# One weight unit converted earlier, two accumulating weight units fewer, and another schedule for the modulation weights, in a four-layer fp32 decoder trunk

## The chip, the cores and the metric

One core of a Trainium2 chip runs the whole program. The metric is device microseconds of one execution. The engines are named as in the profile: PE (TensorE), PEld (its weight loads), DVE (VectorE), ACT (ScalarE), POOL (GpSimd) and SP (SyncE, which here issues most of the DMAs).

## What is computed

`x` is (1, 256, 1024) in float32, `c` is (1, 1024). Four layers, each a token mixer followed by a causal convolution FFN; the mixers are gMLP, latent attention (MLA), HGRN2 (a gated recurrence) and gMLP again.

```
mod = silu(c) @ ada_w[l] + ada_b[l]           # 6 x 1024 per layer: shift, scale, gate, twice
h = rmsnorm(x, mix_norm_g[l]) * (1 + scale1) + shift1
x = x + gate1 * mixer(h)
h = rmsnorm(x, ffn_norm_g[l]) * (1 + scale2) + shift2
x = x + gate2 * ((silu(gate) * val) @ w_down)   # gate, val = split(conv3(h @ w_up))
# gMLP: z = gelu(h @ w_in); u, v = split(z); v = layernorm(v)
#       y = u * (tril(w_s) @ v + b_s); out = y @ w_out
# HGRN2: q, f, i, g = split(h @ w_in); chunked gated recurrence over q, 1-f, i; rmsnorm * silu(g); @ w_o
```

The result is rmsnorm of the last x.

## The kernel before, in words

**Products.** Every large product runs on PE as three fp32r matmuls: the weight is split into `wh` (the fp32r rounding) and `wl` (the rest), the activation into `hh` and `hlo`, and wh·hh, wl·hh and wh·hlo are summed (`mm3`, L252). Weights come in units of 128x2048 floats (1 MB). SP issues each unit's DMA (L190) into one of five `raw` buffers in the order of a list (`plan`), and `conv_half` (L194) splits it by halves: ACT casts a half to `wh` (L215), DVE subtracts to get `wl` (L223). The last arguments of `want` mark units as `again`: for the first half of those, no subtract runs on DVE; ACT multiplies by -1 (L220) and POOL issues a DMA that adds the weight again from memory into `wl` (L221, 512 KB). `unit(ahead, more)` (L227) hands the next unit to the product that asks, after issuing DMAs and conversions up to `ahead` (default 3) units on.

**Stages.** The gMLP of layer 0 begins with the first product: eight K chunks, each one `unit(1, 0)`, for three 512-column blocks of v (`proj_tok_first`, L731), whose results go through ACT's Gelu (`sink`, L792); the fourth block of v (units 8 and 9) follows, then squares (L807), a product of the gate weights (`rsum`, L830; `wsp`, L851), the eight u units with the gate products `sv` (L871), and the eight `go` units back to 1024 columns. Each FFN has 22 `up` units and 11 `dn` units. Where a norm follows, the last chunks of the product before it are held back (`tokens`, L632; `out_end`, L611): DVE applies gates and adds to x (`early`, `gated`, L547 and L548), ACT squares, and PE can begin the transposes `xt` (L495) of the next stage when the scaled row is there (`gx`, L483). On DVE's list `early` stands behind the subtracts of the units that were converted ahead. In HGRN2 a chain of eight levels runs on ACT and DVE (`qk`, `hp`, `hs`, L1208 to L1221), whose products `gram` (L1166, 64 short matmuls a level) run on PE between the products of the i and g units, and DVE copies them (L1168).

**Modulation.** `mod` of the later layers is computed in between. A piece (l, u) is 1024 of the 6144 columns and has four quarters of 1 MB. The pieces of the list `ADA_P` go to PE (quarter: DMA L323, 16 matmuls, L337), the others to DVE (DMA L353, two multiply-and-sum instructions, L362). `pace` (L239) sets for each stage two rates from the table `RATE`, (PE, DVE): how many quarters are loaded for each weight unit; `pacing` (L430) loads them, and runs a loaded quarter two units later. Near the end of a product it loads quarters for the norm instead, as many as `GAPS` says, and `modulated` (L524) runs some of them on PE behind the product. All quarters and units go through SP's one list, in the order in which the code was written out.

Of the kernel before, what the change touches and what calls it, by code (L numbers as in the profile page):

```python
# [22 lines left out]
KC = D // P  # L23
# [21 lines left out]
HGF = 1  # L45
HGO = "o0 o1 s0 a0 o2 s1 a1 n0 o3 s2 n1 w0 s3 n2 w1 n3 w2 w3"
HOLD = (3, 4)
ADA_P = [(1, 1), (1, 2), (1, 3), (1, 4), (2, 3), (2, 4), (3, 5)]
ADA_D = [(l, u) for l in range(L) for u in range(6) if (l, u) > (0, 1) and (l, u) not in ADA_P]
RATE = {("mix", 0): (0.05, 0.9), ("u", 0): (0.1, 1.0), ("go", 0): (0.35, 0.5), ("up", 0): (0.1, 0.2),  # L50
        ("dn", 0): (0.0, 0.4), ("mix", 1): (2.0, 0.0), ("up", 1): (0.0, 0.32), ("dn", 1): (0.0, 0.97),
        ("mix", 2): (0.0, 0.0), ("lev", 2): (0.5, 0.0), ("hout", 2): (0.25, 0.0), ("up", 2): (0.0, 0.2),
        ("dn", 2): (0.0, 0.87), ("mix", 3): (0.0, 0.5), ("u", 3): (0.0, 0.6), ("go", 3): (0.0, 0.55),
        ("up", 3): (0.0, 0.0), ("dn", 3): (0.0, 0.0)}
MAGIC = 12582912.0
TWO_PI = 2.0 * math.pi
# [35 lines left out]
def build(ctx, tc, A, out, stages=None):  # L92
# [62 lines left out]
    i = act.activation(cact[:], cin[:], AF.Silu)  # L155
# [15 lines left out]
    def want(aps, again=()):  # L171

        plan.extend((*a, i in again) for i, a in enumerate(aps))
# [53 lines left out]
    def unit(ahead=None, more=DMA_AHEAD):  # L227
        u = state["use"]
        ahead = state["ahead"] if ahead is None else ahead
        while state["dma"] < min(len(plan), u + ahead + (more if u else 0)):  # L230
            dma_next()
        while state["conv"] < min(len(plan), u + ahead) or halves:
            conv_half()
        state["use"] += 1
        r = ready.pop(0)
        pacing()
        return r

    def pace(kind, l, left=None, tag=None):  # L239
        state["rate"] = dict(zip("pd", RATE[kind, l]))  # L240
        state["gap"] = GAPS[2 * l + (kind in ("up", "dn"))]
        if left is not None:
            state["left"] = left
        if tag is not None:
            state["tag"] = tag
# [72 lines left out]
    def ada_tensor(l, u):  # L318


        def load(i):
            raw = ada_tile(f"adaw{l}_{u}_{i}", (P, 2, 4, 256))
            nc.sync.dma_start(raw[:].rearrange("p a b c -> p (a b c)"), A["adap"][ADA_P.index((l, u)), i])  # L323

            def run():
                h = ADA_P.index((l, u)) % 2
                ps = adaps[:, h, :]
# [44 lines left out]
    firsts = {}  # L372
# [358 lines left out]
    def proj_tok_first(name, sink, start=None):  # L731

        nb = 3 if start else 2
        ps = [(acc if i < 4 else misc)(f"{name}{i}") for i in range(2 * nb)]

        def part(w, b, e):
            return w[b // 2][e][:, b % 2 * 512 : b % 2 * 512 + 512]

        def chunk(kc):
            if start:  # L740
                firsts["w"] = unit(1, 0)
            elif kc % 2 == 0:
                firsts["w"] = unit(2)
            with contextlib.ExitStack() as es:
                if start and kc < KC - 1:
                    es.enter_context(tc.issue_after(firsts["pe"]))
                w = firsts["w"] if start else firsts["w"][kc % 2 :]
                if not start:
                    if kc:
                        low(kc - 1, firsts["wp"])  # L750
                    firsts["wp"] = w
                for b in range(nb):
                    for t in range(2):
                        for e in range(2):
                            i = pe.matmul(ps[2 * b + t][:], hh[:, kc, t * P : t * P + P], part(w, b, e), start=kc == 0 and e == 0, stop=False)  # L755
                if start or kc == KC - 1:
                    i = low(kc, w)
            firsts["pe"] = state["mm"] = getattr(i, "ins", i)

        def low(kc, w):  # L760
            for b in range(nb):
                for t in range(2):
                    i = pe.matmul(ps[2 * b + t][:], hlo[:, kc, t * P : t * P + P], part(w, b, 0), start=False, stop=kc == KC - 1)
            return i

        if start:
            start(chunk)
        else:
            for kc in range(KC):
                chunk(kc)  # L770
        for i in range(2 * nb):
            sink(i // 2, i % 2, ps[i])
# [324 lines left out]

    def hg_units():
        for n in ("hg_f", "hg_q", "hg_i", "hg_g", "hg_o"):
            want([(A[n][i], 2048) for i in range(4)], {"hg_f": (0, 1), "hg_i": range(4), "hg_g": range(4)}.get(n, ()))  # L1100

    def hg_bounds():
        lbp = prm[:, col("lb") : col("lb") + 32].rearrange("p (d h) -> p d h", d=4)
# [280 lines left out]
    for t in range(2):  # L1384
        act.activation(ss0[:, 6 + t : 7 + t], ss0[:, t : t + 1], AF.Sqrt, bias=epsc[:], scale=1.0 / D)
        scaled(t, root(t, ss0[:, 6:8]))
    for m, units in (("p", ADA_P), ("d", ADA_D)):
        for l, u in units:
# [61 lines left out]
def pack(i):  # L1450
# [36 lines left out]
    ap = aw.reshape(L, 4, 2, P, 6, 8, 4, 32)  # L1487
    r["adap"] = np.stack([ap[l, :, :, :, u].transpose(0, 2, 1, 4, 3, 5).reshape(4, P, 2048) for l, u in ADA_P])

# [52 lines left out]
```

## Time and profile before

| | |
|---|---|
| median of 3 runs | 1368.1 us (1364.61, 1368.1, 1368.23) |
| the profiled execution, and its span | 1369.07 us, 1367.3 us |
| PE busy | 1323.5 us (97%) |
| DVE, ACT, POOL busy | 1105.1, 799.6, 37.7 us |
| DMA | 340.16 MB, 249 GB/s on average |
| mean granted PE clock | 0.989 |

PE is busy nearly throughout, so what it waits for, and where its clock is at half, is read place by place. The stages begin at about (us from the span's start): first product 13, u 76, go 132, up of layer 0 185, dn 324, MLA 380, up of layer 1 472, dn 599, HGRN2 670, up of layer 2 829, dn 973, gMLP of layer 3 1022, up 1173, dn 1299.

### The profile page before, as it was taken

How to read it: one execution, taken by the hardware profiler on the slowest of the kernel's cores; microseconds unless marked ns; L12 is line 12 of the kernel's file. 1: busy time of each engine (PE TensorE's matmuls, PEld its weight loads, DVE VectorE, ACT ScalarE, POOL GpSimd, SP SyncE). 2: the span in 40 equal slices, each digit the busy share in tenths (PEclk: the TensorE clock that was granted, in tenths of full speed). 3: DMA queues.
4: the chain of work that ended last, by engine and by line, in shares of the span. 5: the costliest groups of instructions: out<-in, count | busy, mean ns of one | idle time of the engine just before them, and what ended most of it. 6: DMA issues, size and time to landing. Idle time of an engine off the chain costs nothing. (4 is left out here: it accounts for less than half of the span.)

```text
span 1367.3 us, 25166 instructions
## 1 busy us (share of the span) xinstructions
PE 1323.5 (97%) x10197; PEld 1202.2 (88%) x10197; DVE 1105.1 (81%) x1851; ACT 799.6 (58%) x1252; POOL 37.7 (3%) x47
## 2 busy tenths in 40 slices
PE   8999989999999999999898999999999999999997
PEld 7789889998878799988796879999778998999986
DVE  4499869899776689899866867899988896888874
ACT  4664456665376666653596556666455754666652
POOL 0000000000000000000011000000000000000000
PEclk9999999999999999999999999999999999999999
DMA  9868976666985466589769474657878589355550
GB/s 374 314 231 302 382 252 224 230 221 230 397 312 205 151 217 232 204 339 374 273 202 297 136 244 147 217 208 295 321 295 328 209 312 367 118 178 184 200 200 31
DMA packets 52188, 340.16 MB, mean 249 GB/s; under 512 B 6884, under 2 KB 8036, under 8 KB 13926
## 3 DMA queue, kind: packets, MB, share of 16 engines
q1 hardware_dynamic: 48320, 326.95, 63.8%
q0 software_dynamic: 2592, 9.44, 3.7%
q10 hardware_dynamic: 1160, 2.17, 0.5%
q8 instruction: 80, 1.31, 0.4%
q14 instruction: 36, 0.29, 0.1%
HBM read 337.45 MB, written 1.08 MB: 248 GB/s over the span
## 5 line engine op out<-in xcount | busy, mean ns | idle before, releaser
L215 ACT CAST wh<-raw 128x1024 fp32r<-128x1024 f32 (+1 forms) x422 | 429.4, 1041 | 323.7 <-PE up L706 89.3
L223 DVE TENSOR_TENSOR wl<-raw,wh 128x1024 fp32r<-128x1024 f32 (+1 forms) x404 | 483.5, 1213 | 105.8 <-ACT wh L215 105.3
L705 PE MATMUL up<-hh,wh 128*128 128x256 f32 x1280 | 314.2, 283 | 0.0
L706 PE MATMUL up<-hlo,wh 128*128 128x256 f32 x1280 | 314.1, 283 | 0.0
L705 PEld LDWEIGHTS up<-hh,wh 128*128 128x128 f32 x1280 | 245.7, 192 | 0.4 <-ACT y L1334 0.4
L706 PEld LDWEIGHTS up<-hlo,wh 128*128 128x128 f32 x1280 | 245.7, 192 | 0.0
L709 PE MATMUL up<-hh,wl 128*128 128x256 f32 x1280 | 179.8, 283 | 0.0
L709 PEld LDWEIGHTS up<-hh,wl 128*128 128x128 f32 x1280 | 165.1, 192 | 0.4 <-issue 0.4
L362 DVE CUSTOM_DVE_ANT_0 adaw<-adaw,cbc,prm 128x1024 f32<-128x1024 f32 x120 | 151.2, 1279 | 5.3 <-DMA adaw<-adad 5.3
L254 PE MATMUL dn<-wl,gh 128*128 128x512 f32 x339 | 133.3, 393 | 2.3 <-DVE wl L223 2.3
L1334 ACT ACTIVATE y<-up,cwb 128x256 f32<-128x256 f32 x176 | 98.8, 561 | 60.4 <-DVE y L1336 60.4
L253 PE MATMUL dn<-wh,gh 128*128 128x512 f32 x339 | 130.1, 390 | 1.4 <-DVE y L1336 1.3
L255 PE MATMUL dn<-wh,gl 128*128 128x512 f32 x339 | 131.0, 389 | 0.0
L1335 DVE SCALAR_TENSOR_TENSOR y<-up,cwb,y 128x255 f32<-128x255 f32 x176 | 84.4, 479 | 25.6 <-ACT y L1334 25.0
L1336 DVE SCALAR_TENSOR_TENSOR y<-up,cwb,y 128x254 f32<-128x254 f32 x176 | 84.0, 477 | 1.4
L254 PEld LDWEIGHTS dn<-wl,gh 128*128 128x128 f32 x339 | 63.6, 188 | 19.0 <-DVE wl L223 6.4
L253 PEld LDWEIGHTS dn<-wh,gh 128*128 128x128 f32 x339 | 63.7, 188 | 15.2 <-ACT warm L630 1.7
L255 PEld LDWEIGHTS dn<-wh,gl 128*128 128x128 f32 x339 | 63.7, 188 | 12.9
L705 PE MATMUL u<-hh,wh 128*128 128x256 f32 x256 | 64.5, 290 | 0.0
L706 PE MATMUL u<-hlo,wh 128*128 128x256 f32 x256 | 62.9, 283 | 0.0
L653 ACT CAST gh<-g 128x256 fp32r<-128x256 f32 x88 | 35.3, 401 | 37.2 <-DVE g L1341 36.6
L654 DVE TENSOR_TENSOR gl<-g,gh 128x256 fp32r<-128x256 f32 x88 | 37.1, 422 | 20.7 <-ACT gh L653 18.7
(388 smaller groups left out, 2258.2 us busy)
## 6 DMA issues: line engine op xcount, KB each, us to landing
raw<-up SPq DMA_DIRECT2D x88, 1024.0 KB
adaw<-adad SPq DMA_DIRECT2D x60, 1024.0 KB
raw<-dn SPq DMA_DIRECT2D x44, 1024.0 KB
adaw<-adap SPq DMA_DIRECT2D x28, 1024.0 KB
raw<-gmu SPq DMA_DIRECT2D x16, 1024.0 KB
raw<-gmo SPq DMA_DIRECT2D x16, 1024.0 KB
raw<-gmv SPq DMA_DIRECT2D x8, 1024.0 KB
adaf<-ada SPq DMA_DIRECT2D x7, 1024.0 KB
```

The source lines that it names most:

```text
L215: act.copy(wh[:, :w], raw[:, o : o + w])
L223: i = dve.tensor_tensor(wl[:, :w], raw[:, o : o + w], wh[:, :w].bitcast(F32), op=ALU.subtract)
L253: pe.matmul(ps, lh, rh, start=start, stop=False)
L254: pe.matmul(ps, lh, rl, start=False, stop=False)
L255: i = pe.matmul(ps, ll, rh, start=False, stop=stop)
L362: r = dve.tensor_tensor_reduce(raw[:, e, :], raw[:, e, :], cbc[:], 1.0, prm[:, c0 : c0 + 1], ALU.mult, ALU.add, mod[:, l, b : b + 1])
L705: pe.matmul(ps[:, g, :], a, src_h(k), start=k == 0, stop=False)
L706: pe.matmul(ps[:, g, :], a, src_l(k), start=False, stop=False)
L709: i = pe.matmul(ps[:, g, :], b, src_h(k), start=False, stop=k == nk - 1)
L1334: act.activation(y[:], ps[:, e, :], AF.Identity, bias=b, scale=w[2])
L1335: dve.scalar_tensor_tensor(y[:, 1:], ps[:, e, : S - 1], w[1], y[:, 1:], op0=ALU.mult, op1=ALU.add)
L1336: dve.scalar_tensor_tensor(y[:, 2:], ps[:, e, : S - 2], w[0], y[:, 2:], op0=ALU.mult, op1=ALU.add)
```

## The change

It does five things. The last K chunk of the first product calls `unit(3)`, so units 9 and on are loaded and converted with it. The HGRN2 units hg_i and hg_g are no longer `again`. Piece (1, 1) goes from `ADA_P` to DVE. `RATE` loads more DVE quarters in the up stages and the dn stage of layer 0, and fewer in the dn stages of layers 1 and 2. The PE rate in the up stage of layer 0 and in the output of HGRN2 is 0.

```diff
-ADA_P = [(1, 1), (1, 2), (1, 3), (1, 4), (2, 3), (2, 4), (3, 5)]
+ADA_P = [(1, 2), (1, 3), (1, 4), (2, 3), (2, 4), (3, 5)]
...
-RATE = {("mix", 0): (0.05, 0.9), ("u", 0): (0.1, 1.0), ("go", 0): (0.35, 0.5), ("up", 0): (0.1, 0.2),
-        ("dn", 0): (0.0, 0.4), ("mix", 1): (2.0, 0.0), ("up", 1): (0.0, 0.32), ("dn", 1): (0.0, 0.97),
-        ("mix", 2): (0.0, 0.0), ("lev", 2): (0.5, 0.0), ("hout", 2): (0.25, 0.0), ("up", 2): (0.0, 0.2),
-        ("dn", 2): (0.0, 0.87), ("mix", 3): (0.0, 0.5), ("u", 3): (0.0, 0.6), ("go", 3): (0.0, 0.55),
+RATE = {("mix", 0): (0.05, 0.9), ("u", 0): (0.1, 1.0), ("go", 0): (0.35, 0.5), ("up", 0): (0.0, 0.32),
+        ("dn", 0): (0.0, 0.55), ("mix", 1): (2.0, 0.0), ("up", 1): (0.0, 0.38), ("dn", 1): (0.0, 0.75),
+        ("mix", 2): (0.0, 0.07), ("lev", 2): (0.5, 0.0), ("hout", 2): (0.0, 0.0), ("up", 2): (0.0, 0.32),
+        ("dn", 2): (0.0, 0.65), ("mix", 3): (0.0, 0.5), ("u", 3): (0.0, 0.6), ("go", 3): (0.0, 0.55),
...
-                firsts["w"] = unit(1, 0)
+                firsts["w"] = unit(1, 0) if kc < KC - 1 else unit(3)
...
-            want([(A[n][i], 2048) for i in range(4)], {"hg_f": (0, 1), "hg_i": range(4), "hg_g": range(4)}.get(n, ()))
+            want([(A[n][i], 2048) for i in range(4)], (0, 1) if n == "hg_f" else ())
```

Where it moves instructions is read from the order in which each engine's list is written out. On ACT, at the end of the first product (`wh8`, `wh9` are the halves of units 8 and 9, `v0_166<-v0_169` and on are the Gelu sinks, `jk` the squares), before:

```order
L215 CAST wh8_0_780<-raw8_772 128x1024
L215 CAST wh8_1024_784<-raw8_772 128x1024
L792 ACT_TABLE_LOAD
L792 ACTIVATE v0_166,vsum_168<-v0_169 128x512
L792 ACTIVATE v1_167,vsum_168<-v1_170 128x512
...
L807 ACTIVATE jk_760,ss_747<-v1_167,nsh_746 128x512
L820 DMA ws_765<-gmws 128x1024
L823 DMA bs_767<-gmbs 1x1024
L215 CAST wh9_0_788<-raw9_774 128x1024
L215 CAST wh9_1024_792<-raw9_774 128x1024
```

and with the change:

```order
L215 CAST wh8_0_728<-raw8_714 128x1024
L215 CAST wh8_1024_732<-raw8_714 128x1024
L792 ACT_TABLE_LOAD
L792 ACTIVATE v0_166,vsum_168<-v0_169 128x512
L215 CAST wh9_0_736<-raw9_716 128x1024
L215 CAST wh9_1024_740<-raw9_716 128x1024
L792 ACTIVATE v1_167,vsum_168<-v1_170 128x512
```

The two casts of unit 9 move from behind five sinks, six squares and two DMA issues to behind the first sink. DVE's two subtracts of unit 9 move likewise, ahead of the sums at L810, and two of unit 12's move behind `wsp`.

On SP, at the end of the dn product of layer 0, from the last dn unit but one to the first units of MLA (`adaw_u_i` is quarter i of piece (1, u); `adap` rows are for PE, `adad` rows for DVE), before:

```order
L190 DMA raw_3885<-dn 128x2048
L323 DMA adaw_2_3_3895<-adap 128x2048
L353 DMA adaw_0_1_3673<-adad 128x2048
L353 DMA adaw_0_2_3779<-adad 128x2048
L323 DMA adaw_2_0_3781<-adap 128x2048
L323 DMA adaw_2_1_3817<-adap 128x2048
L353 DMA adaw_0_3_3857<-adad 128x2048
L323 DMA adaw_2_2_3859<-adap 128x2048
L190 DMA raw_3921<-dn 128x2048
L190 DMA raw_3959<-mla_a 128x2048
L190 DMA raw_3981<-mla_a 128x2048
```

and with the change:

```order
L190 DMA raw_3873<-dn 128x2048
L323 DMA adaw_3_1_3887<-adap 128x2048
L353 DMA adaw_0_3_3623<-adad 128x2048
L353 DMA adaw_1_0_3695<-adad 128x2048
L353 DMA adaw_1_1_3731<-adad 128x2048
L323 DMA adaw_2_2_3769<-adap 128x2048
L353 DMA adaw_1_2_3807<-adad 128x2048
L323 DMA adaw_2_3_3809<-adap 128x2048
L323 DMA adaw_3_0_3847<-adap 128x2048
L353 DMA adaw_1_3_3885<-adad 128x2048
L190 DMA raw_3913<-dn 128x2048
L190 DMA raw_3949<-mla_a 128x2048
```

Nine quarters stand ahead of the last dn unit where seven stood; the ninth uses the buffer of the third DVE quarter (1_1), so its issue waits for that quarter's two instructions on DVE.

On SP at the end of the dn product of layer 1, up to HGRN2's first unit, before:

```order
L190 DMA raw_6975<-dn 128x2048
L353 DMA adaw_1_3_6947<-adad 128x2048
...
L190 DMA raw_7017<-dn 128x2048
L323 DMA adaw_3_0_6949<-adap 128x2048
L353 DMA adaw_2_0_6987<-adad 128x2048
L323 DMA adaw_3_1_6989<-adap 128x2048
L353 DMA adaw_2_1_7030<-adad 128x2048
L323 DMA adaw_3_2_7032<-adap 128x2048
L190 DMA raw_7058<-dn 128x2048
L353 DMA adaw_2_2_7070<-adad 128x2048
L190 DMA raw_7096<-dn 128x2048
L353 DMA adaw_2_3_7108<-adad 128x2048
L190 DMA raw_7136<-hg_f 128x2048
```

and with the change:

```order
L190 DMA raw_6970<-dn 128x2048
L353 DMA adaw_2_0_6983<-adad 128x2048
...
L323 DMA adaw_3_3_6985<-adap 128x2048
L190 DMA raw_7013<-dn 128x2048
L353 DMA adaw_2_1_7023<-adad 128x2048
L323 DMA adaw_4_0_7025<-adap 128x2048
L190 DMA raw_7051<-dn 128x2048
L353 DMA adaw_2_2_7063<-adad 128x2048
L190 DMA raw_7089<-dn 128x2048
L190 DMA raw_7127<-hg_f 128x2048
```

Five quarters stand between these units where eight stood. The table of rates also takes the two PE quarters out of the up stage of layer 0, and the two PE quarters that ran in the norm ahead of the up stage of layer 3 run in the gMLP norm before it. On DVE the change adds eight subtracts in HGRN2 and eight multiply-and-sum instructions in all; POOL issues eight accumulating DMAs fewer, ACT eight multiplications fewer. Of the four added subtracts of hg_g, three stand on DVE's list between the first `qk` operation of the second level and the second `gram` copy, counting one that moved there from behind the first copy, and one stands between the second and the third copy.

## Rows read from the trace of the kernel before

**Rows 1.** The page's list of busy time: engine, us (share of the span), instructions.

```profile
PE 1323.5 (97%) x10197; PEld 1202.2 (88%) x10197; DVE 1105.1 (81%) x1851; ACT 799.6 (58%) x1252; POOL 37.7 (3%) x47
```

**Rows 2.** The waits of PE over the whole run: what waited, what ended the wait, us in total, times, longest.

```profile
PE xt L495 <- DVE gx L483: 6.7, 3, 4.2
PE gram L1166 <- issue: 6.1, 2, 4.9
```

**Rows 3.** Table by stretch: start and end, length, busy us of PE, PEld, DVE, ACT and POOL, then the granted PE clock, the DMA share and GB/s.

```profile
78.00:139.00 61.00, 59.82 (x473) 58.24 (x472) 60.94 (x106) 28.98 (x39) 0.00 (x0) 1.00 0.79 276
137.00:173.00 36.00, 36.00 (x162) 29.85 (x161) 28.05 (x36) 16.42 (x17) 2.05 (x2) 1.00 0.99 384
180.90:187.70 6.80, 5.71 (x27) 5.63 (x28) 5.80 (x17) 6.06 (x14) 0.00 (x0) 0.50 1.02 381
191.00:324.00 133.00, 133.00 (x1089) 129.71 (x1088) 113.98 (x198) 80.74 (x130) 1.01 (x3) 1.00 0.61 221
344.00:363.00 19.00, 19.00 (x86) 15.73 (x85) 14.01 (x21) 4.48 (x5) 0.00 (x0) 1.00 1.01 426
380.60:387.40 6.80, 6.78 (x63) 5.82 (x64) 6.04 (x16) 6.74 (x12) 0.00 (x0) 1.00 1.01 423
484.00:598.00 114.00, 114.00 (x952) 114.00 (x951) 103.31 (x177) 76.69 (x121) 0.13 (x1) 1.00 0.66 244
669.00:675.80 6.80, 5.83 (x27) 5.66 (x28) 5.82 (x17) 6.08 (x14) 0.13 (x1) 0.50 0.36 108
750.90:754.30 3.40, 1.63 (x63) 1.33 (x67) 0.63 (x2) 0.00 (x0) 0.62 (x1) 0.50 0.78 277
```

**Rows 4.** PE's timeline, the rows that begin after a wait, and the last of the first product: start, length, line, out<-in, count, the idle time before and what ended it.

```profile
66.89 0.73 PE L253 MATMUL v<-wh,hh 128*128 128x512 f32 x2 [2.85 <-ACT wh L215]
68.16 0.74 PE L254 MATMUL v<-wl,hh 128*128 128x512 f32 x1 [0.53 <-DVE wl L223]
...
74.88 1.88 PE L830 MATMUL rsum<-ws,ones 128*128 128x512 f32 x4
...
181.99 3.65 PE L495 MATMUL xt<-ident,gx 128*128 128x128 f32 x16 [5.05 <-DVE ss L475]
...
380.55 2.21 PE L495 MATMUL xt<-ident,gx 128*128 128x128 f32 x16 [2.06 <-DVE gx L483]
...
669.97 2.43 PE L495 MATMUL xt<-ident,gx 128*128 128x128 f32 x10 [4.20 <-DVE gx L483]
...
752.67 0.91 PE L1166 MATMUL gram<-qk 128*32 128x32 f32 x50 [4.90 <-issue]
...
1170.81 1.94 PE L495 MATMUL xt<-ident,gx 128*128 128x128 f32 x16 [0.52 <-DVE ss L475]
```

**Rows 5.** The first product's end: ACT's casts of units 9 to 12, and DVE's subtracts; then DVE ahead of the norm before the up stage of layer 0.

```profile
65.81 7.67 ACT L215 CAST wh<-raw 128x1024 fp32r<-128x1024 f32 x8
...
66.87 11.04 DVE L223 TENSOR_TENSOR wl<-raw,wh 128x1024 fp32r<-128x1024 f32 x8 [5.41 <-ACT wh L215]
...
172.46 1.22 DVE L223 TENSOR_TENSOR wl<-raw,wh 128x1024 fp32r<-128x1024 f32 x1 [1.61 <-ACT wh L215]
173.60 0.68 DVE L547 TENSOR_TENSOR early<-go,gx 128x512 f32<-128x512 f32 x1
```

**Rows 6.** One PE quarter between matmuls of the up stage of layer 0 (PE's timeline), and the DVE instruction of a quarter (the page's group: count, busy us, mean ns).

```profile
238.36 1.07 PE L337 MATMUL adaps<-adaw,cact 128*32 128x256 f32 x16
239.36 0.39 PE L705 MATMUL up<-hh,wh 128*128 128x256 f32 x1
...
L362 DVE CUSTOM_DVE_ANT_0 adaw<-adaw,cbc,prm 128x1024 f32<-128x1024 f32 x120 | 151.2, 1279 | 5.3 <-DMA adaw<-adad 5.3
```

**Rows 7.** The end of dn of layer 0: SP's issues, ACT's casts of the last dn unit and the two mla_a units, and DVE up to `early`.

```profile
340.30 0.33 SPq L323 DMA_DIRECT2D adaw<-adap  x1
...
351.90 0.36 SPq L190 DMA_DIRECT2D raw<-dn  x1
...
363.68 2.00 ACT L215 CAST wh<-raw 128x1024 fp32r<-128x1024 f32 x2 [10.50 <-DMA raw<-dn]
...
368.63 2.01 ACT L215 CAST wh<-raw 128x1024 fp32r<-128x1024 f32 x2 [0.44 <-DMA raw<-mla_a]
...
371.99 0.68 DVE L547 TENSOR_TENSOR early<-dn,gx 128x512 f32<-128x512 f32 x1
```

**Rows 8.** The end of dn of layer 1: ACT's casts of the last dn unit but one and of the first hg_f unit, and DVE's `early`.

```profile
644.99 2.00 ACT L215 CAST wh<-raw 128x1024 fp32r<-128x1024 f32 x2 [10.88 <-DMA raw<-dn]
...
654.71 1.05 ACT L215 CAST wh<-raw 128x1024 fp32r<-128x1024 f32 x1 [2.85 <-DMA raw<-hg_f]
...
661.68 0.68 DVE L547 TENSOR_TENSOR early<-dn,gx 128x512 f32<-128x512 f32 x1
```

**Rows 9.** HGRN2: the DMA queues from 747 to 750.5 us (packets, MB, share of 16 engines; the software queue is POOL's), and DVE's copies of the second and third gram.

```profile
q0 software_dynamic: 102, 0.37, 54.2%
...
q8 instruction: 1, 0.02, 1.7%
...
753.67 0.73 DVE L1168 COPY_PREDICATED haa<-gmask,gram 128x512 f32<-128x512 uint8 x1 [2.93 <-PE gram L1166]
761.32 0.74 DVE L1168 COPY_PREDICATED haa<-gmask,gram 128x512 f32<-128x512 uint8 x1 [3.43 <-PE gram L1166]
```

**Rows 10.** PE's timeline at the second wait of gram.

```profile
760.35 0.93 PE L1166 MATMUL gram<-qk 128*32 128x32 f32 x85 [1.19 <-issue]
```

## The prediction

> **What bounds the kernel now.** I read the busy times first: PE works 1323.5 us of the span of 1367.3 [rows 1]. Less PE work, or less waiting of PE, is all that can save time, so the next view is the list of PE's waits. Its longest entries are transposes `xt` that wait at norms (6.7 us for `gx` in three waits, one of 4.2) and short `gram` matmuls (6.1 us in two, one of 4.9) with "issue" as releaser, which is a wait for nothing that a semaphore shows [rows 2]. PE's timeline gives each its place [rows 4]. Then the table by stretch shows what a long wait costs afterwards and which resource is full [rows 3]: after waits of 5.05 and 4.20 us the granted clock is 0.50 (1.2 GHz) for 6.8 us, in which PE is busy 5.71 and 5.83 us; after the wait of 2.06 us at the MLA norm it is 1.00 (2.4 GHz). 5.8 us of work at half rate is 2.9 us at the full one, so **a long norm wait costs its length and 2.9 us more**.
>
> All sums are against the profiled execution, 1369.07 us, which lies 1.0 above the median of 1368.1; the forecast is given against the median. About 0.3% (4.1 us) is what a measurement of this kernel can tell from no change.
>
> **The first product.** PE waits 2.85 us for `wh` and 0.53 for `wl` of unit 9 there, and runs seven matmuls at half rate until 71.7 [rows 4]: 0.2 us each, so 4.8 us in all. With unit 9's casts behind the first sink both waits go. The two casts still cost ACT 1.9 us (7.67 for eight [rows 5]), now ahead of the other sinks, the squares and the DMA of the gate weights, so `rsum` becomes ready later on ACT's and POOL's side and part of the gain waits there. Further on DVE decides: it is busy 60.94 of 61.00 us over the u stage [rows 3]. Its list loses only what moves into earlier idle time: two of the eight subtracts that run from 66.87 (11.04 us, 1.38 each), 2.8 us, into the 5.41 us it idled [rows 5]; unit 12's two only move behind `wsp`. Then the DMAs are full (0.99 busy, 137 to 173 us [rows 3]), and the norm ahead of `up` waits 5.05 us for DVE, whose `early` starts right behind a subtract that waited for ACT [rows 4, 5]. So PE's 4.8 us don't pass through; DVE's 2.8 less some of ACT's delay do. I take **-2**, bounds -1 and -4.8.
>
> **Piece (1, 1) on DVE.** Two PE quarters leave the up stage of layer 0, where PE is busy 133.00 of 133.00 us [rows 3]. One is 1.0 us (16 matmuls from 238.36 to the next row at 239.36 [rows 6]): **-2.0**, near certain. The other two leave the wait ahead of the last up stage, which lengthens from 0.52 us [rows 4] to about 2.5. That lies between 2.06 (clock stayed full) and 2.85 (it fell): 0, or some 1.5 if the clock falls as in the 3.4 us stretch at `gram` (1.63 us of work in it [rows 3]). I take +0.5. The eight DVE instructions (1.28 us, 10.2 in all [rows 6]) lie in the up stages with the ones that the rates move there, next to a DVE that is busy 113.98 of 133.00 and 103.31 of 114.00 us [rows 3]: nothing, as long as each finds its gap (a rival below says what if not).
>
> **The MLA norm (end of dn, layer 0).** This is the term against the change. From 340.30 SP issues quarters behind the last dn unit but one; the last dn unit's DMA is issued at 351.90 and ACT can cast it only at 363.68, after 10.50 us of waiting [rows 7]. The DMA engines are full meanwhile: 426 GB/s at a share of 1.01 [rows 3]. Eight loads in turn (seven quarters and the unit), 1.05 MB each, take 2.46 us apiece at that rate. With the change nine quarters go ahead, **two more: +4.9 us** for that unit and for the two mla_a units behind it. SP's ninth quarter waits for DVE's third; six loads are queued at once and two follow as DVE frees buffers, so the queue doesn't run dry and the two loads are the price. `early` stands on DVE's list behind the subtracts of the second mla_a unit (cast at 368.63, `early` at 371.99 [rows 7]), so it moves from 372.0 to about 376.9 and `xt` from 380.55 to 385.5, while PE ends its dn work about when it did, some 0.5 us later for the last unit's `wl`. PE's wait grows from 2.06 to more than 6 us, and then the clock is at half after it: +2.9. In sum **+7.8**. The bounds: 0, if the loads find the queue emptier than now, and +8.5.
>
> **The HGRN2 norm (end of dn, layer 1)** is the counterpart. ACT waits there 10.88, 2.86 and 2.85 us for DMAs, the last for hg_f at 654.71, and `early` follows the conversion at 661.68 [rows 8]. Between the same units now stand five quarters instead of eight: 7.4 us less ahead of hg_f. `xt` can't follow PE's last dn matmul by less than about the 2.06 us of the MLA norm, so the wait of 4.20 [rows 4] shrinks by 2.1, and the 2.9 us at half clock go: **-5.0**, bounds -2 and -6.
>
> **HGRN2's levels.** Eight multiplications on ACT and eight accumulating DMAs go, eight subtracts come. PE stands 4.90 us inside one level's `gram` matmuls, then runs at half clock until 754.3 [rows 3, 4]. No semaphore releases it, and the packet of the instruction queue moved in that stretch, while POOL's queue held 54.2% of the engines' time [rows 9]. The next such wait is 1.19 us [rows 10], so a fetch beside less traffic costs about that: 3.7 us may go, and 1.6 at half clock. But the levels are a chain through DVE: of the added subtracts two new ones and a moved one stand ahead of the second `gram` copy, one ahead of the third (1.2 us each), and DVE's waits there were 2.93 and 3.43 us [rows 9]. They fit, and leave PE at most what DVE's waits had over: 6.4 - 3.6 = 2.8, of which I take **-2**; bounds 0 and -3.6. The rule that speaks against this stands in the Trainium skill, "DMA: Bandwidth & Descriptors", section "Queues, rings and completion order": an engine goes round its queues packet by packet. By the row, POOL's 102 packets took 0.3 us each (54.2% of 16 times 3.5 us), so by that rule a fetch loses about 0.3 us to them and not 3.7; the sum would be without these -2.
>
> **Sum:** -2 - 2.0 + 0.5 + 7.8 - 5.0 - 2 = -2.7 from 1369.07, or **1365.4 us** against the median.
>
> **The rivals.**
> 1. *The MLA norm isn't later.* The queue at 340 may be emptier than before, since the stage's other quarters come earlier in it, or DVE's order lets the unit through. For: the share of the whole list decides, and dn's rate only rises from 0.4 to 0.55. Against: nine loads are in the list ahead of one. Without the 7.8: 1357.6.
> 2. *PE's first gain passes whole.* If DVE in the u stage follows PE: 2.8 us more, 1362.6. Against: 60.94 of 61.00.
> 3. *The gram wait stays* (what moves it is not POOL's traffic): 1367.4. For: the packets' size above. Against: where the engines are less loaded the waits are 1.2.
> 4. *DVE becomes the bound of the up stages: slower.* The rates put about 2.6, 1.3 and 2.6 quarters more into the three up stages (22 units times the change of the rate). A quarter holds DVE 2.4 us at a stretch. In layer 1 DVE's spare time is 10.7 of 114 us over some 20 units, 0.5 us a unit with the present quarters. If each added quarter holds `wl` or the gates back by 1.2 us, PE waits 6.5 times 1.2 = 7.8 us: 1373.2. It decides where a subtract comes later than PE's next unit. Against: PE is busy 114.00 of 114.00 us there with a rate of 0.32 already, and 0.38 leaves a quarter every 2.6 units.
>
> **How the numbers follow.** Forecast 0.42; its own range is 1361 to 1370, a good quarter of it faster by over 0.3% (below 1364.0), the rest no change. Rival 1 0.20 (faster), rival 2 0.10 (mostly faster), rival 3 0.14 (no change), rival 4 0.14 (slower by over 0.3%, above 1372.2, except for a little). Faster 0.40, same 0.47, slower 0.13. The range takes in rivals 1 and 4: 1357 to 1374.
>
> **What would show it.** No wait at v, and `rsum` some 5 us earlier but `early` of layer 0 only 2; a wait of over 6 us for `xt` at the MLA norm with half clock after it and one near 2 at HGRN2's without; a gram wait near 1.2; no L337 between 191 and 324. Wrong if the last dn unit of layer 0 is cast no later after its predecessors than now, or if PE waits for `wl` in the up stages.

## The result, and the profile after

| | before | with the change |
|---|---|---|
| median of 11 runs | 1368.1 us (1364.61 to 1369.79) | 1373.15 us (1369.53 to 1377.4) |
| ratio, 95% interval | | 1.0047 [1.0033, 1.0061] |
| profiled execution, span | 1369.07, 1367.3 us | 1377.32, 1375.6 us |

The change makes the kernel slower by some 0.5%. The profiled execution of the change lies 4.2 us above its median, that of before 1.0 above its own, so sizes read from the two traces are in sum some 3 us too large; where a size matters, a timed run stands behind it.

The busy times first, which answer to [rows 1]:

```profile
PE 1323.9 (96%) x10133; PEld 1202.6 (87%) x10133; DVE 1127.3 (82%) x1873; ACT 792.1 (58%) x1244; POOL 30.5 (2%) x39
```

PE has 64 instructions fewer and no less busy time: more of its work ran at half clock (mean granted clock 0.986 against 0.989). DVE has 22 us more. The waits of PE (what waited, what ended it, us in total, times, longest) answer to [rows 2]:

```profile
PE dn L254 <- DVE wl L223: 10.2, 13, 2.0
PE xt L495 <- DVE ss L475: 8.1, 3, 5.2
PE xt L495 <- DVE gx L483: 5.3, 2, 4.9
PE up L709 <- DVE wl L223: 2.6, 4, 1.1
PE gram L1166 <- issue: 2.5, 1, 2.5
PE rsum L830 <- POOL ws L826: 1.8, 1, 1.8
```

The wait of `gram` has shrunk from 6.1 us in two to 2.5 in one. Two entries are new in size: PE waits 10.2 us for `wl` in the dn stages (2.3 in five waits before) and 2.6 in the up stages (none before). PE's timeline has the places, and answers to [rows 4] (start, length, count, the wait before and what ended it):

```profile
73.48 3.78 PE L830 MATMUL rsum<-ws,ones 128*128 128x512 f32 x4 [1.83 <-POOL ws L826]
184.35 3.65 PE L495 MATMUL xt<-ident,gx 128*128 128x128 f32 x16 [5.24 <-DVE ss L475]
387.74 3.71 PE L495 MATMUL xt<-ident,gx 128*128 128x128 f32 x16 [4.91 <-DVE gx L483]
611.97 0.50 PE L254 MATMUL dn<-wl,gh 128*128 128x512 f32 x1 [1.52 <-DVE wl L223]
615.18 0.47 PE L253 MATMUL dn<-wh,gh 128*128 128x512 f32 x1 [1.12 <-DVE y L1336]
619.05 0.80 PE L254 MATMUL dn<-wl,gh 128*128 128x512 f32 x1 [2.00 <-DVE wl L223]
680.31 1.97 PE L495 MATMUL xt<-ident,gx 128*128 128x128 f32 x16
1177.53 2.49 PE L495 MATMUL xt<-ident,gx 128*128 128x128 f32 x16 [2.38 <-DVE ss L475]
```

The MLA norm waits 4.91 us, HGRN2's (680.31) not at all, the last FFN norm 2.38. New is the stretch from 611 to 619, the start of dn of layer 1. The table by stretch of the change, in the columns of [rows 3]; its rows are up of layer 0, the end of dn of layer 0, the MLA norm, up of layer 1, the border of up and dn of layer 1, and HGRN2's norm:

```profile
193.00:315.00 122.00, 122.00 (x1019) 122.00 (x1018) 107.40 (x184) 77.41 (x122) 0.73 (x3) 1.00 0.60 220
346.00:365.00 19.00, 19.00 (x85) 15.73 (x85) 16.51 (x26) 4.59 (x6) 0.00 (x0) 1.00 1.01 427
387.70:394.50 6.80, 6.76 (x35) 6.59 (x36) 5.86 (x16) 6.46 (x12) 0.12 (x1) 0.56 0.94 387
494.00:608.00 114.00, 112.63 (x936) 112.19 (x935) 104.17 (x178) 74.15 (x118) 0.13 (x1) 1.00 0.65 243
600.00:622.00 22.00, 17.17 (x107) 14.70 (x106) 21.20 (x36) 9.59 (x17) 0.00 (x0) 0.93 0.99 385
680.30:687.10 6.80, 6.80 (x62) 6.80 (x59) 5.70 (x16) 6.41 (x12) 0.13 (x1) 1.00 0.43 154
```

And the border of up and dn of layer 1 in the kernel before:

```profile
590.00:612.00 22.00, 20.04 (x121) 16.49 (x120) 21.52 (x39) 9.96 (x19) 0.00 (x0) 1.00 0.93 361
```

This row decides how the added quarters are to be priced. Over the whole up stage DVE was busy 103.31 of 114.00 us [rows 3] and seemed to have room; in the 22 us around its end it was busy 21.52 already, and PE had lost 2 us. With the change PE loses 4.8. DVE's timeline of the change shows what stands there:

```profile
600.85 0.48 DVE L1336 SCALAR_TENSOR_TENSOR y<-up,cwb,y 128x254 f32<-128x254 f32 x1
601.24 1.28 DVE L362 CUSTOM_DVE_ANT_0 adaw<-adaw,cbc,prm 128x1024 f32<-128x1024 f32 x1
...
602.78 1.28 DVE L362 CUSTOM_DVE_ANT_0 adaw<-adaw,cbc,prm 128x1024 f32<-128x1024 f32 x1
...
613.36 1.28 DVE L362 CUSTOM_DVE_ANT_0 adaw<-adaw,cbc,prm 128x1024 f32<-128x1024 f32 x1
...
614.95 1.28 DVE L362 CUSTOM_DVE_ANT_0 adaw<-adaw,cbc,prm 128x1024 f32<-128x1024 f32 x1
...
617.78 1.21 DVE L223 TENSOR_TENSOR wl<-raw,wh 128x1024 fp32r<-128x1024 f32 x1
```

Two whole quarters run back to back with the gates `y` and the subtracts, 12 us apart; PE's matmul at 619.05 is the one that waits 2.00 us for the subtract of 617.78.

Where the time went, by stage: lengths worked out from the first row of each stage in PE's timeline (us; the last four columns are experiments, below):

| from, to | before | change | up_rates_only | before_small_ttr | small_ttr | again_dn1_early |
|---|---|---|---|---|---|---|
| first product to FFN 0 norm | 168.33 | 169.67 | 168.22 | 164.18 | 161.46 | 170.62 |
| FFN 0 norm to dn 0 | 133.52 | 130.64 | 133.69 | 131.04 | 128.66 | 132.24 |
| dn 0 to MLA norm | 65.04 | 72.75 | 67.55 | 62.68 | 67.37 | 64.92 |
| MLA norm to FFN 1 norm | 88.00 | 89.55 | 89.13 | 87.84 | 89.13 | 89.59 |
| FFN 1 norm to dn 1 | 130.78 | 132.76 | 130.97 | 130.78 | 130.77 | 130.79 |
| dn 1 to HGRN2 norm | 70.64 | 70.26 | 74.10 | 66.10 | 63.12 | 66.31 |
| HGRN2 norm to FFN 2 norm | 158.98 | 151.33 | 157.06 | 157.56 | 150.85 | 150.74 |
| FFN 2 norm to dn 2 | 128.58 | 130.28 | 128.57 | 128.58 | 128.49 | 128.58 |
| dn 2 to gMLP norm | 64.69 | 67.31 | 68.27 | 62.42 | 63.15 | 64.13 |
| FFN 3 norm to dn 3 | 128.50 | 130.05 | 128.50 | 128.49 | 128.49 | 128.48 |

A norm is its `xt`; the stage left out, the gMLP of layer 3, differs by 0.3 us. The change gains 7.65 us in HGRN2 and 2.9 in up of layer 0, and loses more than that in the other up and dn stages. The first row spreads by itself: again_dn1_early has 170.62 us there and leaves that stretch as it was before, so the change's 1.3 us are no effect that can be told. Two starts of the list of stages further above are put right by these lengths: in the kernel before, dn of layer 0 begins at 315.5 us and dn of layer 2 at 957.5, not at 324 and 973. The row 191 to 324 of [rows 3] so holds 8.5 us of dn.

At the first product the wait at v is gone and `u` begins at 71.26 where it began at 76.19, but DVE is no earlier. POOL's, DVE's and ACT's timelines of the change:

```profile
63.51 2.30 POOL L816 PARTITION_BROADCAST Gb<-Gb  x1 [62.48 <-DMA Gb<-gmg]
71.80 1.63 POOL L826 TENSOR_SCALAR_AFFINE_SELECT ws<-ws 128x1024 f32<-128x1024 f32 x1 [5.99 <-DMA ws<-gmws]
...
64.08 1.75 DVE L811 TENSOR_SCALAR nsh<-nsh 128x2 f32<-128x2 f32 x1
71.24 5.36 DVE L223 TENSOR_TENSOR wl<-raw,wh 128x1024 fp32r<-128x1024 f32 x3 [5.41 <-ACT wh L215]
...
70.18 3.87 ACT L215 CAST wh<-raw 128x1024 fp32r<-128x1024 f32 x4
```

DVE's `nsh`, which took 0.17 us at 61.30 before, takes 1.75 at 64.08 while POOL's broadcast runs; ACT's squares wait for it, and behind them stand ACT's casts of unit 10 (70.18). So DVE idles 5.41 us once more, as it did in the kernel before ahead of unit 9's subtracts at 66.87 [rows 5], and unit 10's subtracts begin at 71.24 where they began at 70.06. The gate weights, whose DMA is issued behind the squares, reach POOL late, and `rsum` waits.

### The profile page after: what moved, and what is told of

It is laid out like the page before. It is cut to its first block, busy times and chain, and to the rows that moved or that the text cites. A ratio compares the mean times of both kernels' runs of the same rounds, so it can differ in the third digit from the quotient of the medians.

```text
span 1375.6 us, 25021 instructions
## 1 busy us (share of the span) xinstructions
PE 1323.9 (96%) x10133; PEld 1202.6 (87%) x10133; DVE 1127.3 (82%) x1873; ACT 792.1 (58%) x1244; POOL 30.5 (2%) x39
## 4 chain that ended last, share of the span: by engine, by line
PE 79%; DVE 13%; ACT 4%; issue 2%; DMA 2%; SPq 0%; POOL 0%; ACTq 0%; DVEq 0%
PE up L706 11%; PE up L705 11%; PE up L709 10%; PE dn L254 4%; PE dn L255 4%; PE dn L253 4%; DVE wl L223 3%; PE v L755 3%; DVE adaw L362 2%; DVE x L548 1%; PE u L706 1%; PE u L705 1%; PE u L709 1%; ACT wh L215 1%; PE xt L495 1%
## 5 line engine op out<-in xcount | busy, mean ns | idle before, releaser
L223 DVE TENSOR_TENSOR wl<-raw,wh 128x1024 fp32r<-128x1024 f32 (+1 forms) x412 | 494.0, 1214 | 106.8 <-ACT wh L215 106.5
L362 DVE CUSTOM_DVE_ANT_0 adaw<-adaw,cbc,prm 128x1024 f32<-128x1024 f32 x128 | 163.7, 1294 | 5.0 <-DMA adaw<-adad 5.0
L254 PE MATMUL dn<-wl,gh 128*128 128x512 f32 x339 | 134.4, 396 | 10.2 <-DVE wl L223 10.2
L1335 DVE SCALAR_TENSOR_TENSOR y<-up,cwb,y 128x255 f32<-128x255 f32 x176 | 84.3, 479 | 25.4 <-ACT y L1334 24.8
```

What stands on the lines that cost most here:

```text
L223: i = dve.tensor_tensor(wl[:, :w], raw[:, o : o + w], wh[:, :w].bitcast(F32), op=ALU.subtract)
L254: pe.matmul(ps, lh, rl, start=False, stop=False)
L362: r = dve.tensor_tensor_reduce(raw[:, e, :], raw[:, e, :], cbc[:], 1.0, prm[:, c0 : c0 + 1], ALU.mult, ALU.add, mod[:, l, b : b + 1])
L1335: dve.scalar_tensor_tensor(y[:, 1:], ps[:, e, : S - 1], w[1], y[:, 1:], op0=ALU.mult, op1=ALU.add)
```

## Experiments

A ratio is to runs of the kernel before on the same chip. Chips differ a little: its medians there were 1365.5 to 1367.7 us.

### The parts by themselves

**again_only**: the kernel before with one line of the change.

```diff
-want(..., {"hg_f": (0, 1), "hg_i": range(4), "hg_g": range(4)}.get(n, ()))
+want(..., (0, 1) if n == "hg_f" else ())
```

> The kernel before with hg_i and hg_g no longer accumulated by DMA, nothing else changed. Theory A (the accumulating DMAs hold up PE's instruction fetch and slow HGRN2, whatever else is changed): the waits of PE for 'issue' in gram and hg, 6.8 us before, fall under 3, HGRN2 from its first xt to the xt after it is about 5 us shorter (it was 7.65 shorter with the whole change, of which about 2.7 is the half clock after the norm), total 4 to 6 us faster. Rival B (the gain in HGRN2 came from the schedule: fewer quarters loaded ahead, other places in the instruction stream): the waits stay at 6 to 7 us and the total is within 2 us of before.

Measured 1363.54 us, ratio 0.9972 [0.9962, 0.9983]: 3.8 us faster by the ratio. Its PE waits:

```profile
PE gram L1166 <- issue: 2.6, 2, 2.4
```

**first_only**: the kernel before with `unit(3)` at the last K chunk.

> The kernel before with unit(3) in the last K chunk, nothing else changed. Theory A (PE's gain at v is taken back within the u stage by VectorE, whose chain up to wsp is no earlier): v to u 6 us shorter, u to go 5 us longer, first up norm 0 to 2.5 us later than before, total between 0 and 3 us slower. Rival B (the 2.4 us by which that norm was later in the whole change came from another schedule of the quarters): the norm is 2 us earlier and the total 1 to 3 us faster, as I had predicted for this part.

Measured 1368.87 us, 1.001 [0.9998, 1.0021]: no gain. **sched_only**: the kernel before with `RATE` and `ADA_P` of the change.

> The kernel before with the new table of rates and piece (1,1) on VectorE, nothing else changed. Theory A (the schedule is what costs: VectorE falls behind in the up stages so that PE waits for wl at the start of each dn, and two more loads stand ahead of the last dn unit at the MLA norm): PE's waits for wl in dn about 10 us against 2.3 before, xt of the MLA norm waits 4 to 6 us, total 4 to 9 us slower. Rival B (those waits need the other parts too): total within 2 us of before.

Measured 1376.05 us, 1.0073 [1.0058, 1.0089], 10 us slower by the ratio, and `wl` waits in dn of 10.1 us in 13, as with the change. The three parts add up: 0.73 - 0.28 + 0.1 = 0.55%, against 0.47%. The loss is the schedule's.

**up_rates_only**: the kernel before with nothing but the three DVE rates of the up stages.

```diff
-("up", 0): (0.1, 0.2) ... ("up", 1): (0.0, 0.32) ... ("up", 2): (0.0, 0.2)
+("up", 0): (0.1, 0.32) ... ("up", 1): (0.0, 0.38) ... ("up", 2): (0.0, 0.32)
```

> The kernel before with only the three VectorE rates of the up stages raised (0.2, 0.32, 0.2 to 0.32, 0.38, 0.32); the dn rates and the pieces stay. Theory A (quarters in the up stages push VectorE behind): PE waits for wl at the starts of dn and in up rise from 2.3 to over 7 us in all, total 3 to 7 us slower unless a shorter norm gives some back. Rival B (the waits at dn come from the dn rates and the quarters that run there, the up stages take these quarters for nothing): waits for wl under 4 us, total same or faster.

Measured 1377.64 us, 1.0085 [1.0069, 1.01]. Its PE waits:

```profile
PE xt L495 <- DVE gx L483: 12.6, 3, 6.3
PE dn L254 <- DVE wl L223: 5.5, 7, 1.3
```

The rates alone cost as much as the whole schedule, but not in the up stages (130.97 and 128.57 in the table): in the dn stages behind them, and more at the norms (12.6 us, from 6.7) than at `wl`. How DVE's lag gets to a norm is seen at HGRN2's. SP's waits from 634 to 652 us, at the end of dn of layer 1, hold this one (what waited, what ended it, us in total, times, longest):

```profile
SPq L285 <- DVE grow L282: 6.3, 1, 6.3
```

L285 is the issue of a gate row, which DVE has to finish first (`grow`), and here it stands on SP's list ahead of the last dn unit. That unit is issued at 647.57, 44.7 us after the first dn matmul; in the kernel before, without such a wait there, it is issued at 638.64, 39.3 us after it.

### Is it DVE's time?

**small_ttr** and **before_small_ttr**: the change, and the kernel before, with the multiply-and-sum on 256 of a quarter's 1024 columns. Three quarters of the modulation products on DVE are left out; all DMAs and instruction counts stay.

```diff
-dve.tensor_tensor_reduce(raw[:, e, :], raw[:, e, :], cbc[:], ...)
+dve.tensor_tensor_reduce(raw[:, e, :256], raw[:, e, :256], cbc[:, :256], ...)
```

> The changed kernel with each multiply-and-sum of a VectorE quarter on 256 of its 1024 columns; three quarters of these products are left out, the loads, the instructions and their order stay. Theory A (VectorE's time for the quarters is what PE waits for at the starts of dn and in up): PE's waits for wl in dn and up fall from 12.8 us to under 3, while the wait at the MLA norm stays at 4 to 6 us, since the loads ahead of the last dn unit are the same; total 8 to 13 us below the changed kernel, 1361 to 1366. Rival B (the waits come from the loads, which hold raw buffers and SP's list): the waits for wl stay above 8 us, total within 3 us of the changed kernel.

> The kernel before with each multiply-and-sum of a VectorE quarter on 256 of its 1024 columns; three quarters of these products are left out. With it the changed kernel fell from 1373.15 to 1344.35. Theory A (the change's loss is VectorE's time: where that is cheap, the change is a gain): the kernel before falls less, to 1350 to 1358, so that with cheap quarters the change is 6 to 13 us faster, not 5 slower. Rival B (cheap quarters help both alike, and the loss lies in loads and waits that stay): the kernel before falls to 1338 to 1344, and the change stays slower.

Measured 1344.35 us, 0.9833 [0.9818, 0.9848], and 1350.22 us, 0.9887 [0.9872, 0.9902]. The instruction of small_ttr, from its page:

```profile
L362 DVE CUSTOM_DVE_ANT_0 adaw<-adaw,cbc,prm 128x256 f32<-128x256 f32 x128 | 58.0, 477 | 7.7 <-DMA adaw<-adad 7.7
```

and its waits of PE, where none for `wl` is left among the longest:

```profile
PE xt L495 <- DVE gx L483: 5.5, 2, 5.0
PE xt L495 <- DVE ss L475: 3.7, 3, 2.7
PE gram L1166 <- issue: 3.4, 2, 2.4
```

**With a short instruction the sign turns**: the same edit makes the kernel 0.54% faster (0.9833 against 0.9887), where it is 0.47% slower with the long one. So what turns the edit's gain into a loss is DVE's time: with the same DMAs in the same order, and a short instruction, the edit gains. Both kernels fell by more than PE's waits for `wl` had been, the change by more than either theory said. One loss stays at the MLA norm, a wait of 5.0 us, and 67.37 us from dn 0 to that norm against 62.68 (in the table): that one isn't DVE's arithmetic.

### The MLA norm

**two_loads_fewer**: the change with two quarters fewer loaded for that norm.

```diff
-GAPS = [2, 4, 3, 3, 2, 2, 2, 0]
+GAPS = [2, 2, 3, 3, 2, 2, 2, 0]
```

> The changed kernel with two PE quarters loaded ahead of the MLA norm instead of four (one number of GAPS); the two others are loaded in MLA. Theory A (the two loads ahead of the last dn unit are the price at that norm): the wait of xt there falls from 4.9 us to 2.5 or less, without half clock after it; from the first dn to the up after MLA 6 to 9 us shorter, total 1364 to 1368. Rival B (VectorE's quarters hold early back, not the loads): the wait stays above 4 us, total 1371 to 1375.

Measured 1367.14 us, 0.9996 [0.9986, 1.0006], level with the kernel before: 0.51% back, some 7 us. The row in which SP issues the last dn unit of layer 0, and its `xt`, with no half clock behind it:

```profile
334.82 5.74 SPq L190 DMA_DIRECT2D raw<-dn  x3
...
379.83 2.21 PE L495 MATMUL xt<-ident,gx 128*128 128x128 f32 x16 [1.42 <-DVE gx L483]
```

The stretch from dn 0 to the norm is 67.06 us and the MLA stage 87.71, against 72.75 and 89.55. The edit does more than leave out two loads: the last dn unit, the third of this row, is now issued ahead of all seven quarters, where the change issues it behind nine. So the queue ahead of the last dn unit and the two mla_a units set this norm, and not the quarters' time on DVE, which is the same; what two loads alone are worth is told by this run only together with that move.

**hold_last_ups**: that kernel, and no DVE quarter loaded behind the last five units of the up stages of layers 1 and 2.

```diff
+if c == NF - 5 and l in (1, 2):
+    state["rate"]["d"] = 0.0
```

> two_loads_fewer, in which no VectorE quarter is loaded in the last five units of the up stages of layers 1 and 2; what is left over moves into dn (one to two quarters each). Theory A (VectorE is behind by the end of up because quarters stand among its last gates and subtracts): PE's waits at the start of these two dn stages fall from 3.0 and 3.3 us to under 1.2 each, no half clock there, total 3 to 6 us below two_loads_fewer, 1361 to 1364. Rival B (the lag builds up over the whole stage and can't be taken off in five units): they stay above 2 us each, total within 1.5 us.

Measured 1372.9 us, 1.0051 [1.0033, 1.007]. The waits at the start of dn of layer 1 were hardly lower (1.52, 0.56 and 0.77 us, 2.9 in sum, from 3.2), those of layer 2 fell from 3.3 to 1.9, and the norm of FFN 2 waited 5.77 us. There DVE's `early` waited for the DMA of the gate, whose quarters had been put off into HGRN2 (they ran on DVE from 779.71, and the gate row was issued at 804.11):

```profile
818.03 0.69 DVE L547 TENSOR_TENSOR early<-wo,gx 128x512 f32<-128x512 f32 x1 [5.17 <-DMA gx<-gate]
```

The idea that the last quarters of the up stage alone make those waits fails for layer 1 and holds in part for layer 2; a quarter that is put off is paid at the norm that needs it.

### The first product

**first_gb_late**: first_only, with the DMA that feeds POOL's broadcast `Gb` behind the squares. **first_ws_early**: that, with the gate weights' DMA issued on ACT behind unit 9's casts and ahead of the sinks (in both gMLP layers).

```diff
-nc.scalar.dma_start(Gb[0:1, :], A["gmg"][j : j + 1])
+with tc.issue_after(state["sq"]):
+    nc.scalar.dma_start(Gb[0:1, :], A["gmg"][j : j + 1])
...
+with tc.issue_after(state["cast"]):
+    nc.scalar.dma_start(gate["w"][:, 0], A["gmws"][j])
```

> unit(3) alone, with the DMA of Gb issued by ACT behind the squares, so that GpSimd's broadcast of it doesn't run while VectorE computes nsh. Theory A (nsh, 0.17 us before, took 1.75 with the change since it waits for GpSimd's broadcast to end): nsh takes under 0.3, the squares and the DMA of ws come 1.5 us earlier, rsum waits under 1 us, the total is 1 to 2 us below unit(3) alone, 1367 to 1368. Rival B (nsh waits for something else): it still takes over 1 us and the total is as with unit(3) alone.

> The same, and the DMA of ws is issued ahead of the sinks as well, behind the casts of unit 9, so that rsum's input is there some 6 us earlier. Theory A (what takes PE's gain back is rsum and with it wsp, by the late DMA of ws): PE doesn't wait at rsum, wsp is ready 2 to 3 us earlier than with unit(3) alone, the first up norm begins 2 to 3 us earlier, total 3 to 5 us below unit(3) alone, 1364 to 1366. Rival B (VectorE's own work in the u stage sets the norm, whatever rsum does): rsum's wait goes, but the norm moves by under 1 us and the total by under 1.5.

Measured 1367.09 us, 0.9995 [0.9983, 1.0006], and 1364.1 us, 0.9979 [0.997, 0.9989]. DVE's timeline of first_gb_late:

```profile
62.71 0.17 DVE L812 TENSOR_SCALAR nsh<-nsh 128x2 f32<-128x2 f32 x1
```

So the broadcast held `nsh`: 1.75 us beside it, 0.17 away from it. In first_ws_early no wait of `rsum` is left, but the length from the first product to the FFN norm is 167.95 us (168.33 before). Its 0.2% are not from there. The gMLP of layer 3, which has the same edit, was 1.1 us shorter (147.46 from its norm to the next, where it had 148.59); where the rest comes from is not shown.

### HGRN2's norm, and a version faster than both

**again_dn1**: again_only with two rates of the change, and **joined**: that with first_ws_early.

```diff
-("dn", 1): (0.0, 0.97) ... ("mix", 2): (0.0, 0.0)
+("dn", 1): (0.0, 0.75) ... ("mix", 2): (0.0, 0.07)
```

> The kernel before without the accumulation of hg_i and hg_g, and with the two rates of the change around HGRN2's norm (dn of layer 1: 0.97 to 0.75, HGRN2: 0 to 0.07); the up rates stay. Theory A (loads ahead of hg_f made that norm wait; the change's wait there vanished because of these two rates): the wait of xt falls from 4.2 us to under 2.2 and no half clock follows, total 3 to 5 us below again_only, 1358 to 1361. Rival B (it vanished since PE came later to that norm, held up by its own waits at the start of dn): the wait stays above 3 us, total within 1.5 us of again_only.

> The parts that gained, in one kernel: no accumulation of hg_i and hg_g, the two rates around HGRN2's norm, unit(3) with ws's DMA ahead of the sinks and Gb's behind the squares; up rates and pieces as before. If the parts add (each is another stage): 4.1 for the accumulation, 3.6 for the first product's version, 3 to 5 for the norm, together 1355 to 1358. If they don't, because DMA-bound norms take each gain back: 1360 to 1364.

Measured 1364.6 us, 0.999 [0.9979, 1.0002], and 1362.67 us, 0.9978 [0.9965, 0.999]. From dn 1 to the norm again_dn1 needs 66.37 us instead of 70.64, and no half clock follows. But the gain is paid back at the next norm, FFN 2:

```profile
821.61 3.65 PE L495 MATMUL xt<-ident,gx 128*128 128x128 f32 x16 [5.46 <-DVE amul L272]
```

With a rate of 0.07 the quarter `adaw_2_3` (quarter (2, 3) in the expectations), the last of the gate that this norm needs, was loaded only behind the third `hg_o` unit (744.19). The gate row was then issued at 799.60, and `early` waited for its way back:

```profile
813.09 0.69 DVE L547 TENSOR_TENSOR early<-wo,gx 128x512 f32<-128x512 f32 x1 [4.73 <-DMA gx<-gate]
```

**again_dn1_early** and **joined_early** differ from these two in one number: it is loaded behind `hg_q`.

```diff
-("mix", 2): (0.0, 0.07)
+("mix", 2): (0.0, 0.3)
```

> The kernel before with hg_i and hg_g not again, the rate of the dn stage of layer 1 at 0.75 as in the change, and the rate ahead of HGRN2's levels at 0.3, so that quarter (2, 3) of the modulation is loaded behind the last hg_q unit and not behind the third hg_o unit. Theory A (the norm of HGRN2 gave its gain back only because that late quarter was run at the next norm): the wait of xt at the norm ahead of the up stage of layer 2 is under 1.5 us, no half clock there, and the time is 1355 to 1359 us where the kernel before is 1367. Theory B (the quarter's two DVE instructions among HGRN2's products and levels cost as much there, since the levels are a chain through DVE): the norm's wait goes, HGRN2 is 3 us longer or more than with hg_i and hg_g alone (153.5 us), and the time stays at 1362 or over.

> The kernel of the other run with the first product's parts joined to it: the last K chunk by unit(3), the gate weights' DMA ahead of the sinks, the broadcast behind the squares. If the parts are worth what each was by itself (0.1% to 0.2% for these) it is 1 to 3 us below the other run: 1353 to 1358 by theory A, 1360 to 1362 by theory B. If the first product's gain is lost at the norm ahead of the up stage of layer 0, the two runs are within 1 us.

Measured 1357.56 us, 0.9946 [0.9933, 0.9959], and 1356.51 us, 0.9926 [0.9912, 0.9939]. The norm in again_dn1_early:

```profile
817.98 1.98 PE L495 MATMUL xt<-ident,gx 128*128 128x128 f32 x16 [0.52 <-DVE ss L475]
```

The late quarter alone had taken the gain. One part of the change and fewer quarters ahead of HGRN2's norm, without the up rates, are worth 0.54%. Joined with the first product's parts it is 0.74%, the fastest version run here; the 0.2% between the two is at the edge of the intervals.

## Why the prediction was wrong

The forecast was 2.7 us faster; it came 5 us slower. By its steps:

- **The step that failed: the quarters in the up stages, "nothing, as long as each finds its gap".** The forecast's terms for the schedule sum to -2.0 + 0.5 + 7.8 - 5.0 = +1.3; sched_only measured 0.73%, +10. The average over the up stage (103.31 of 114.00 busy) hid that DVE was full around its end (21.52 of 22.00) and owed gates and subtracts to the next stage. The backlog comes out behind the up stages: as `wl` waits in dn (10.2 us) and at norms. The prediction's own sign of being wrong, PE waiting for `wl` in the up stages, came too (2.6 us). That it is DVE's time is shown by the pair with the short instruction, and that the up rates alone suffice by up_rates_only (0.85%); which quarters cost most is not settled, since hold_last_ups mostly moved the wait.
- **Rival 4 is what happened, in its sign and its size (1373.2 against 1373.15), but not in its place.** It put 6.5 waits of 1.2 us into the up stages; PE waits there 2.6 us. The chance of 0.14 rested on PE's 114.00 of 114.00 in the up stage, which says nothing of the stage behind it. The size is partly luck: the other terms were off too.
- **The MLA norm, +7.8: the two loads right, the sum near by luck.** The same steps that [rows 7] show of before, in the timelines of SP, ACT and DVE of the change:

```profile
342.41 0.33 SPq L323 DMA_DIRECT2D adaw<-adap  x1
...
361.02 0.42 SPq L190 DMA_DIRECT2D raw<-dn  x1
...
370.50 1.99 ACT L215 CAST wh<-raw 128x1024 fp32r<-128x1024 f32 x2 [15.21 <-PE dn L255]
...
379.19 0.68 DVE L547 TENSOR_TENSOR early<-dn,gx 128x512 f32<-128x512 f32 x1
```

  From the first quarter's issue to the cast it is 28.1 us where it was 23.4: 4.7 more for two loads, against 4.9. The page puts ACT's wait down to PE, which had long been done; a DMA issued at 361.02 is the later one. But the stretch grew by 7.7 us and the stage behind it by 1.6, together 9.3. Of the 7.7, 2.6 are a term that the forecast lacked: the first quarter is issued 27.4 us after the first dn matmul, where it was 24.8. With the short instruction the stretch grows by 4.7 only (62.68 to 67.37), which fits that these 2.6 are DVE's time. So PE too was later, and its wait is 4.91, not over 6. two_loads_fewer takes back 5.7 us ahead of the norm and 1.8 behind it.

  The half clock was priced too high and laid to the change alone. The MLA stage takes 87.7 to 88.0 us in the runs whose clock stayed full behind this norm, and 89.1 to 89.6 where it fell: 1.1 to 1.9 us, not 2.9. And it fell in most kernels that leave this norm as it was, as in again_only (`xt`, and a row of its table by stretch):

```profile
379.43 2.94 PE L495 MATMUL xt<-ident,gx 128*128 128x128 f32 x16 [1.91 <-DVE gx L483]
...
380.60:387.40 6.80, 6.80 (x53) 6.08 (x52) 6.54 (x17) 6.23 (x11) 0.00 (x0) 0.75 1.01 413
```

  That the profiled execution of the kernel before kept its full clock after 2.06 us [rows 4] was one outcome of two, and the forecast took it for the rule.
- **HGRN2's norm, -5.0: right by itself, lost in company.** With the change its wait and half clock are gone, as forecast, but from dn 1 to the norm it is 70.26 against 70.64 us, since PE waits 4.6 us at 611 to 619. The rate alone, with its late quarter put right, takes 4.3 us off that stretch, and not 2.1: in again_dn1_early `xt` doesn't wait at all, so the floor of 2.06 us under this wait was wrong. The half clock behind this norm is worth some 2.8 us, near the 2.9 (HGRN2 takes 153.52 us in again_only, where the clock fell, and 150.74 in again_dn1_early).
- **HGRN2's levels, -2: the direction right, the size too small, the mechanism only in part shown.** again_only is 3.8 us faster (0.28% [0.17, 0.38]); the bound was -3.6. The waits fell from 6.1 to 2.6 us, and the chain through DVE took less of it than I let it. The Trainium skill's rule on queues served round by packet ("DMA: Bandwidth & Descriptors", "Queues, rings and completion order") would, by the prediction's estimate, have left the waits within about 0.3 us of where they were; the traces do not agree with that estimate. In every run with the accumulating DMAs of hg_i and hg_g the longest wait of `gram` is 4.0 to 4.9 us, in every run without them 2.0 to 2.5. What the short matmuls wait for is still not shown, nor that it is a fetch, so the rule itself is not tested.
- **The first product, -2: wrong, there is no gain.** PE's waits went, and `rsum` had new ones on POOL's side, as named; but of DVE's 2.8 us nothing passes (first_only 167.83 us to the norm against 168.33, and 1.001 [0.9998, 1.0021] in all). The step that failed here is that the two subtracts would move into DVE's idle time of 5.41 us: they did, but ACT casts unit 10 only behind the squares, so the same idle time opened again behind them. `nsh` beside the broadcast adds 1.6 us to it, but undoing that (first_gb_late) gave a gain that is not clear of the noise. What holds the u and go stages is DVE: with the short instruction the same stretch takes 161.46 us with the change and 164.18 without, one trace of each.
- **Piece (1, 1): right.** Up of layer 0 is 2.9 us shorter in the two traces (forecast 2.0); against other kernels that leave this stage as it was, at 132.2 us and more, it is 1.6 or more. The last FFN norm waits 2.38 us and half clock follows, so that up stage takes 1.55 us longer: the upper of the two cases between which 0.5 was taken.

## What to carry to other kernels

Before work is put next to a busy engine at no cost, look at the last 20 us of that stage and the first of the next one, not at the average: a backlog is paid behind the stage that made it, and through a list such as SP's it holds up loads that have nothing to do with it. Cheap versions of the suspect, in both kernels, tell an engine's time from DMAs and order in two runs. When a load is thinned out at one deadline, find the next deadline that now forces it; one rate made 0.1% into 0.5%.

## What the runs showed of the hardware

A `TENSOR_SCALAR` of 128x2 on DVE took 1.75 us while POOL's partition broadcast ran (63.51 to 65.81) and 1.44 in first_only, against 0.17 in the kernel before and with the broadcast moved away. After PE's wait of 2.38 us at the last FFN norm the granted clock was 0.50 (1.2 GHz) for 3.4 us, and likewise at 619 us after waits of 1.52, 1.12 and 2.00 within 9 us. The length of the last wait doesn't settle it: at the MLA norm the clock stayed at 1.00 (2.4 GHz) after 2.06 us in the kernel before and 2.35 in hold_last_ups, and was at half for some 3.4 of the next 6.8 us (0.75 on average) after 1.91 in again_only, 1.94 in again_dn1_early and 2.22 in first_only.
